# Two kinds of expert weight blocks taken by turns, with other PSUM homes, in a two-block transformer kernel

## Chip, core and metric

One core of a Trainium2 chip runs the whole program. The metric is device time in microseconds (us), the median of three timed runs. Beside it stands one profiled execution, from which every row below is taken.

## What is computed

Two small transformer blocks, 256 tokens of width 1024, one after the other, all in float32. The part that matters is the mixture of experts at the end of the first block:

```python
def moe_swiglu(h, router_w, w1, w3, w2):          # cut: the sorting of tokens
    top_val, top_idx = lax.top_k(h @ router_w, 2)  # 2 of 8 experts for each token
    gates = softmax(top_val)
    # for every expert e, over the tokens that chose it (xb):
    y = (silu(xb @ w1[e]) * (xb @ w3[e])) @ w2[e]  # 1024 -> 2816 -> 1024
    # each token adds its two y, weighted by its gates
```

Each expert has three matrices of 1024 x 2816 (or its transpose), 34.6 MB in float32, and all eight are read from HBM: 276.8 MB of the kernel's 505 MB.

## The kernel before

**The experts' stage.** Experts are ordered by how many tokens chose them. The first three (`NL = 3`) have slots for 128 tokens and are computed with three products: every weight chunk is split into a rounded part `hi` (ScalarE, L325) and the rest `lo` (VectorE, L326), and TensorE multiplies hi by hi, hi by lo and lo by hi. The other five have slots for 64 tokens and are plain: TensorE reads the float32 chunk as it landed (`raw`), with 64 columns, two tiles of the array at a time.

**Chunks and places.** Weights arrive in chunks of 1 MiB, two DMAs of 512 KB each; an expert is 33 chunks (11 each of w1, w3, w2). A *place* `(e, f)` is one block of columns of one expert. A three-product expert has six places: five of 6 chunks (4 for w1 and w3, 2 for w2), and one of 3. A plain expert has three: two of 12 chunks (8 and 4), and one of 9. `moe_steps()` lists the places in order. For each, `up` multiplies by w1 and w3 (tiles `H`, L1417 or plain L1434), ScalarE and VectorE form the gated product `mg` (L1443, L1444), `gtrans` transposes it on TensorE (`gTp`, L1455 or L1464) and `down` multiplies by w2 into `Y` (L1483) or `Ys` (L1497). The `down` of a place comes after the `up` of the next place, and its `gtrans` between w1 and w3 of the next place.

**Buffers and queues.** `stream()` fixes the order of the chunks; SyncE (SP) issues all their DMAs in that order, each into the next free home. There are 7 homes of one chunk for raw chunks in this stage (3 from the start, 2 + 2 from `more_raw`). A home of a three-product chunk is free when its split is done, that of a plain chunk when TensorE has read it. `hi` and `lo` hold three chunks, and two are split ahead of use (`look = 2`). Once the last three-product chunk (`i_three`) is done with, the `hi` and `lo` buffers too are homes for plain chunks, 6 more. Two further chunks go to tiles that are still unused at the stage's start.

**Background work.** `gather` selects an expert's tokens (tiles `xgp`, `STp`, `gsp`), `gather_plain` those of the five plain experts at once, `combine` and `combine_plain` add an expert's result to the residual `hT` (tile `sc`). They are generators: one step of each active one runs at a `tick`, one tick a chunk or so.

**The turn.** Between the three-product and the plain part stands `moe_rest`, a branch for experts with more tokens than slots, which is not taken here; all engines read a count and pass it.

**PSUM** has 8 banks of 128 x 512 float32: tags `mm` 3, `st` 1, `Y` 2, `ac` 2. A tag without banks of its own (`gT`) falls to `ac`. The instruction order on each engine is that of a scheduler inside the framework, which may place an instruction later than the code has it.

Of the kernel before, what the change touches and what calls it, by code (L numbers as in the profile page):

```python
# [8 lines left out]
F32R = mybir.dt.float32r  # L9
# [8 lines left out]
T = 256  # L18
# [3 lines left out]
NE = 8  # L22

NL = 3
RMS_EPS = 1e-6
LN_EPS = 1e-5
BIG = 1e30
# [29 lines left out]

def moe_steps():

    return [(e, f) for e in range(NL) for f in range(6)] + [(e, f) for e in range(NL, NE) for f in range(3)]  # L60


def up_keys(nm, e, f):
# [13 lines left out]
def stream():  # L77

    ch = []

    def pack(key, nm, i, parts):
        ch.append((key, [128, KD, sum(n for _, n in parts)], [(nm, i, 0, D, c, n) for c, n in parts]))

    def cols(key, nm, i, c0, n=256):
        pack(key, nm, i, [(c0, n)])

    def rows(key, nm, i, r0, n=256):
        ch.append((key, [128, n // 128, D], [(nm, i, r0, n, 0, D)]))  # L90

    for i in range(6):
        cols(("ain", i), "a_w_in", (0,), 256 * i)
    for i in (8, 10, 9, 11, 6, 7):
        cols(("ain", i), "a_w_in", (0,), 256 * i)
    for i in range(4):
        cols(("aout", i), "a_w_out", (0,), 256 * i)
    for f in range(12):
        if f < 11:
            cols(("f1", f), "ffn_w1", (0,), 256 * f)  # L100
            cols(("f3", f), "ffn_w3", (0,), 256 * f)
        if f > 0:
            rows(("f2", f - 1), "ffn_w2", (0,), 256 * (f - 1))
    rows(("pple", 0), "ple_proj", (0,), 0)
    for i in range(4):
        cols(("gple", 0, i), "ple_gate", (0,), 256 * i)
    for i in (4, 5, 6, 7, 0, 1, 2, 3):
        cols(("cin", i), "c_w_in", (0,), 256 * i)
    for i in range(4):
        cols(("cout", i), "c_w_out", (0,), 256 * i)  # L110
    shapes = {c[0]: c[1] for c in experts()}
    prev = None
    for e, f in moe_steps():
        down = down_keys(*prev) if prev else []
        up = up_keys("m1", e, f) + up_keys("m3", e, f)
        ch += [(k, shapes[k[0], k[2], k[3]], None) for k in (down + up if (e, f) == (NL, 0) else up + down)]
        prev = e, f
    ch += [(k, shapes[k[0], k[2], k[3]], None) for k in down_keys(*prev)]
    rows(("pple", 1), "ple_proj", (1,), 0)
    for i in range(4):  # L120
        cols(("gple", 1, i), "ple_gate", (1,), 256 * i)
    for l in range(2):
        for n, parts in enumerate((
                [(512, 128), (704, 128)], [(640, 64), (832, 32), (1504, 12), (384, 128)], [(0, 256)],
                [(256, 128), (1120, 128)], [(864, 256)], [(1248, 64), (1376, 64), (1312, 64), (1440, 64)],
                [(1516, 256)], [(1772, 256)], [(2028, 256)])):
            pack((f"c{n}", l), "w_in_2", (l,), parts)
        for i in range(4):
            cols(("wout", l, i), "w_out_2", (l,), 256 * i)
        for f in range(17):  # L130
            if f < 16:
                cols(("up", l, f), "w_up_2", (l,), 256 * f)
            if f > 0:
                rows(("dn", l, f - 1), "w_down_2", (l,), 256 * (f - 1))
    return ch
# [45 lines left out]
class Prog:  # L181
# [986 lines left out]
    def moe(self, nxt):  # L1168
        nc, a = self.nc, self.a
# [17 lines left out]
        x = self.nx[0:2]  # L1187
# [1 line left out]
        xtk = [self.xt(f"xtk{q}").rearrange("p (s b k) t -> p s b (k t)", s=2, b=2) for q in range(2)]  # L1189

        def rows(s, b, q, f):
            ps = self.ac("xtp", (128, 512), F32R)
            for j in range(4):
                nc.tensor.transpose(ps[:, 128 * j:128 * j + 128], x[s][:, 4 * q + j, 128 * b:128 * b + 128],
                                    self.identr)
            return f(xtk[q][:, s, b], ps.bitcast(F32))
# [152 lines left out]
        def gather(e):  # L1349
            S = slots((e,)) if e else first  # L1350
            last = [None, None]
            g = self.p_x.tile([128, 2, KD, 128], F32R, tag="X", name="xg")
            for i in range(2):
                for s in range(2):
                    ps = self.psum("ac" if s or e else "mm", "xgp", (128, 4, 128))
                    for j in range(4):
                        for b in range(2):
                            nc.tensor.matmul(ps[:, j], xtk[i][:, s, b, 128 * j:128 * j + 128], S[:, b, 0],
                                             start=b == 0, stop=b == 1)
                    o = g[:, s, 4 * i:4 * i + 4]  # L1360
                    if s:
                        last[0] = nc.scalar.activation(o, ps, AF.Copy)
                    else:
                        last[1] = nc.vector.tensor_copy(o, ps)
                    yield
            if not e:
                with self.after(*last):
                    ghl.append(gates())
            ST, gs = slotsT(S, (e,), ghl[0])
            xg[e] = g[:, 0], g[:, 1]  # L1370
            sg[e] = ST[:, 0], gs[:, 0]

        def gather_plain():

            g = self.big("xs", [128, KD, NE - NL, 64])
            for e0 in range(NL, NE, 3):
                es = range(e0, min(e0 + 3, NE))
                n = len(es)
                S = slots(es, plain=True)
                yield  # L1380
                for k in range(KD):
                    ps = self.ac("xgp", (128, n, 64))
                    for s in range(2):
                        for b in range(2):
                            nc.tensor.matmul(ps, xtk[k // 4][:, s, b, 128 * (k % 4):128 * (k % 4) + 128],
                                             S[:, b, :, 0:64], start=s == 0 and b == 0, stop=s == 1 and b == 1)
                    o = g[:, k, e0 - NL:e0 - NL + n]
                    if k % 2:
                        nc.scalar.activation(o, ps, AF.Copy)
                        yield  # L1390
                    else:
                        nc.vector.tensor_copy(o, ps)
                q = slotsT(S, es, ghl[0], f"s{e0}")
                for m, e in enumerate(es):
                    xg[e] = g[:, :, e - NL]
                    sg[e] = q[0][:, m], q[1][:, m]
# [4 lines left out]
        G, Y = {}, {}  # L1401
# [46 lines left out]

        def gtrans(e, f):
            t = G.pop((e, f))  # L1450
            ps = self.psum("gT", "gTp", (128, 4, 128))
            if e < NL:
                nf = 4 if f < 5 else 2
                for j in range(nf):
                    nc.tensor.transpose(ps[:, j], t[:, 128 * j:128 * j + 128], self.ident)  # L1455
                hi = p.tile([128, 4, 128], F32R, tag="gth", name="gth", bufs=2)
                lo = p.tile([128, 4, 128], F32R, tag="gtl", name="gtl", bufs=2)
                self.hilo(hi[:, :nf], lo[:, :nf], ps[:, :nf])
                GT[e, f] = hi, lo
                return  # L1460
            gt = p.tile([128, 4, 128], F32, tag="gth", name="gts", bufs=2)
            for j in range(4):
                c = 128 if f < 2 or j < 2 else 64
                nc.tensor.transpose(ps[:, j, :c], t[:c, 128 * j:128 * j + 128], self.ident[:c, :c])  # L1464
            if f < 2:
                nc.vector.tensor_copy(gt, ps)
            else:
                nc.vector.tensor_copy(gt[:, 0:2], ps[:, 0:2])
                nc.vector.tensor_copy(gt[:, 2:4, 0:64], ps[:, 2:4, 0:64])
            GT[e, f] = gt  # L1470
# [53 lines left out]
        def combine_plain(e):  # L1524
# [4 lines left out]
            nc.scalar.activation(t, Y.pop(e), AF.Identity, scale=gs[:, 0:1])  # L1529
            yield  # L1530
            for i in range(2):
                P = [self.ac("sc", (128, 2, T)) for _ in range(2)]
                for j in range(2):
                    c = 256 * i + 128 * j
                    for q in range(2):
# [11 lines left out]

        prev = None
        for e, f in steps:
            if (e, f) == (NL, 0):  # L1550
                gtrans(*prev)
                down(*prev)
                self.drain()
# [2 lines left out]
                self.moe_rest(xtk, cni, slots, slotsT, ghl[0])  # L1556
                prev = None
            up(e, f, prev)
            if e < NL and f == 1:
                self.add(gather(e + 1) if e < NL - 1 else gather_plain())  # L1560
            if prev:
                down(*prev)
                if f == 0:
                    self.add((combine if e <= NL else combine_plain)(e - 1))
            prev = e, f
        gtrans(*prev)
        down(*prev)
# [4 lines left out]
    def moe_rest(self, xtk, cni, slots, slotsT, ghl):  # L1572
# [4 lines left out]
        with tc.If(n > 128):  # L1577
# [20 lines left out]
            for e, off in [(e, 128) for e in range(NL)] + [(e, o) for e in range(NL, NE) for o in (64, 192)]:  # L1598
                S = slots((e,), off)
                ST, gs = slotsT(S, (e,), ghl)  # L1600
                P = [self.ac("P20"), self.ac("P21")]
                for i in range(2):
                    for j in range(4):
                        for s, ps in enumerate(P):
# [509 lines left out]
    def build(self):  # L2114
# [24 lines left out]
                self.rows = True  # L2139
                self.mods(32)  # L2140
        self.dump("h4", self.hT)
        with self.more_raw("raw3", "left", 2), self.phase("moe", 1, Y=2, ac=2):
            self.moe((self.col("ln_ple", 1),))
        raw2.__exit__(None, None, None)
        self.dump("h5", self.hT)
# [77 lines left out]
```

## Time and profile before

| | |
|---|---|
| median of three runs | 1873.13 us (1872.68 to 1876.75) |
| the profiled execution's own time | 1875.38 us |
| its span, first to last instruction | 1873.6 us |
| experts' stage, first `H` to the last `Ys` matmul | 442.9 to 1162.5 us |
| three-product part of it | 442.9 to 756 us |
| plain part | 762.6 to 1162.5 us |

How to read it: the span is what rows of the trace add up to, the run's own time is 1.8 us more, and the three timed runs lie around it. A matmul's end is modelled, so its busy time overlaps with the next one's; the step from start to start is what one costs.

### The profile page before, as it was taken

What the parts mean: (1) busy time and instruction counts of PE and PEld (TensorE: products, weight loads), DVE (VectorE), ACT (ScalarE), POOL (GpSimd) and SP (SyncE); (2) the same over time, 40 slices, a digit from 0 to 9 for tenths busy, and PEclk for the clock granted to TensorE, in tenths of its full rate; (3) what the DMA queues carried; (4) which work ended last, traced back from release to release, by engine and by line L of the source; (5) the groups of instructions that cost most, each with busy time, mean ns of one, the idle gap of its engine ahead of it and who ended that gap; (6) DMA issues with size and microseconds to landing.
All of it is one profiled execution on the core that took longest, in us unless ns stands there. A gap on an engine that the chain in (4) does not pass through costs nothing.

```text
span 1873.6 us, 31611 instructions
## 1 busy us (share of the span) xinstructions
PE 1768.3 (94%) x11889; PEld 1428.9 (76%) x11889; DVE 1176.8 (63%) x2150; ACT 909.2 (49%) x1428; POOL 53.0 (3%) x93
## 2 busy tenths in 40 slices
PE   7999999999999999899898888999999999999998
PEld 7989999997888888333232223887899998889997
DVE  7888888687899988101000011886888877666554
ACT  6754435666787866000000002666555456666553
POOL 1000000000000000000000000200000000000000
PEclk9999999998999999999999999999999999999999
DMA  8479886575899989999999999443588864326651
GB/s 308 144 261 315 309 308 218 185 246 210 297 361 330 368 299 326 376 413 412 413 412 413 412 413 383 163 155 106 209 307 303 314 215 138 113 69 204 190 185 53
DMA packets 138544, 508.55 MB, mean 271 GB/s; under 512 B 18192, under 2 KB 18832, under 8 KB 137872
## 3 DMA queue, kind: packets, MB, share of 16 engines
q1 hardware_dynamic: 132480, 496.92, 73.0%
q10 hardware_dynamic: 5904, 9.53, 1.6%
q8 instruction: 96, 1.57, 0.3%
q14 instruction: 64, 0.52, 0.1%
HBM read 505.34 MB, written 1.05 MB: 270 GB/s over the span
## 4 chain that ended last, share of the span: by engine, by line
PE 31%; DMA 22%; DVE 4%; ACT 2%; issue 1%; SPq 0%; DVEq 0%; ACTq 0%
DMA raw<-in_moe_dram 19%; PE y L632 8%; PE up L406 7%; PE zp L406 5%; DMA adaw<-in_ada_dram 2%; PE H L1434 2%; PE S L1839 2%; DVE lo L326 1%; PE op L406 1%; PE pTp L1045 1%; PE cmh L1946 1%; PE oT L1873 1%; ACT hi L325 1%; DVE adacc L865 1%; PE op L431 1%
## 5 line engine op out<-in xcount | busy, mean ns | idle before, releaser
L326 DVE TENSOR_TENSOR lo<-raw,hi 128x1024 fp32r<-128x1024 f32 x516 | 621.8, 1223 | 131.5 <-ACT hi L325 130.0
L325 ACT ACTIVATE hi<-raw 128x1024 fp32r<-128x1024 f32 x516 | 530.9, 1054 | 185.6 <-PE H L1417 38.2
L1434 PE MATMUL H<-raw,xs 128*64 128x512 f32 (+1 forms) x960 | 229.7, 567 | 39.3 <-DMA raw<-in_moe_dram 32.7
L1434 PEld LDWEIGHTS H<-raw,xs 128*64 128x64 f32 x960 | 75.1, 137 | 182.7 <-issue 97.8
L1444 DVE SCALAR_TENSOR_TENSOR mg<-H,gs,mg 128x512 f32<-128x512 f32 (+3 forms) x38 | 26.3, 692 | 290.1 <-PE H L1434 198.7
L632 PE MATMUL y<-ghi,hi 128*128 128x256 f32 x688 | 193.6, 283 | 3.9 <-ACT ghi L377 3.7
L632 PE MATMUL y<-ghi,lo 128*128 128x256 f32 x688 | 194.0, 282 | 2.0 <-DVE lo L326 2.0
L632 PE MATMUL y<-glo,hi 128*128 128x256 f32 x688 | 194.0, 282 | 1.9 <-DVE glo L378 1.9
L1417 PE MATMUL H<-hi,xg 128*128 128x512 f32 (+1 forms) x576 | 178.1, 382 | 0.0
L1443 ACT ACTIVATE mg<-H,gs 128x512 f32<-128x512 f32 (+3 forms) x38 | 24.2, 636 | 307.0 <-PE H L1434 306.9
L865 DVE SCALAR_TENSOR_TENSOR adacc<-adaw,cact,adacc 128x768 f32<-128x768 f32 x126 | 130.9, 1039 | 47.7 <-DMA adaw<-in_ada_dram 46.0
L406 PE MATMUL up<-xhi,hi 128*128 128x258 f32 x480 | 136.3, 284 | 0.2 <-ACT hi L325 0.2
L406 PE MATMUL up<-xhi,lo 128*128 128x258 f32 x480 | 135.6, 283 | 0.0
L406 PE MATMUL up<-xlo,hi 128*128 128x258 f32 x480 | 135.4, 282 | 0.0
L632 PEld LDWEIGHTS y<-ghi,hi 128*128 128x128 f32 x688 | 129.9, 189 | 5.0 <-ACT ghi L377 4.9
L632 PEld LDWEIGHTS y<-glo,hi 128*128 128x128 f32 x688 | 130.3, 189 | 2.9 <-DVE glo L378 2.9
L632 PEld LDWEIGHTS y<-ghi,lo 128*128 128x128 f32 x688 | 130.2, 189 | 2.6 <-DVE lo L326 2.6
L1497 PE MATMUL Ys<-raw,gts 128*64 128x512 f32 x440 | 119.4, 606 | 8.6 <-DMA raw<-in_moe_dram 7.1
L1417 PEld LDWEIGHTS H<-hi,xg 128*128 128x128 f32 x576 | 105.9, 189 | 20.7
L1417 PE MATMUL H<-lo,xg 128*128 128x512 f32 (+1 forms) x288 | 108.9, 378 | 0.0
L406 PE MATMUL H<-xhi,lo 128*128 128x256 f32 x336 | 94.7, 282 | 0.0
L406 PE MATMUL H<-xhi,hi 128*128 128x256 f32 x336 | 94.3, 281 | 0.0
(604 smaller groups left out, 3820.2 us busy)
## 6 DMA issues: line engine op xcount, KB each, us to landing
raw<-in_moe_dram SPq DMA_DIRECT2D x524, 512.0 KB, 10.0
raw<-in_stream_dram SPq DMA_DIRECT2D x316, 512.0 KB, 4.5
adaw<-in_ada_dram SPq DMA_DIRECT2D x64, 768.0 KB, 6.4
cw1k<-in_cw1k_dram ACTq DMA_DIRECT2D x2, 1024.0 KB, 6.4
cw1v<-in_cw1v_dram ACTq DMA_DIRECT2D x2, 1024.0 KB, 5.5
raw<-in_stream_dram SPq DMA_DIRECT2D x4, 472.0 KB, 4.5
hT<-in_xT_dram SPq DMA_DIRECT2D x4, 256.0 KB, 7.2
raw<-in_stream_dram ACTq DMA_DIRECT2D x2, 512.0 KB, 7.6
```

What stands on the lines that cost most here:

```text
L325: self.halved = (nc.scalar.activation(hi, raw, AF.Copy), nc.vector.tensor_sub(lo, raw, hi.bitcast(F32)))
L326: nc.vector.tensor_sub(lo, raw, hi.bitcast(F32)))
L406: nc.tensor.matmul(ps, p[:, k, j:j + m], q[:, k, :], start=start and n == 0, stop=n == 3 * nk - 1, skip_group_check=True)
L431: nc.tensor.matmul(ps, p[:, k, c:c + m[n]], q[:, k, :], start=k == i == 0 and not (n and shared), stop=k == KD - 1 and i == 2, skip_group_ ...
L632: self.nc.tensor.matmul(ps, p[:, k, 128 * dt:128 * dt + 128], q[:, k, :], start=f == 0 and n == 0 and dt % 2 == 0, stop=last and n == 5, s ...
L865: nc.vector.scalar_tensor_tensor(acc, w[:, j], self.cact[:, k:k + 1], acc, op0=OP.mult, op1=OP.add)
L1417: nc.tensor.matmul(ps[:, :n], g[s][:, m // 3], w[:, k], start=m == 0, stop=m == 23, skip_group_check=True)
L1434: nc.tensor.matmul(ps[64 * q:64 * q + 64, :c], g[:, k], x[:, kk], start=k == 0, stop=k == KD - 1, skip_group_check=True)
L1443: nc.scalar.activation(t[z, :c], H[0][z, :c], AF.Silu, scale=gs[z, 1:2])
L1444: nc.vector.scalar_tensor_tensor(t[z, :c], H[1][z, :c], gs[z, 1:2], t[z, :c], op0=OP.mult, op1=OP.mult)
L1497: nc.tensor.matmul(Y[e][64 * q:64 * q + 64], gt[:, kk, 64 * n:64 * n + 64], w[:, k, 512 * q:512 * q + 512], start=key[2] == 0 and kk == 0, ...
L1839: nc.tensor.matmul(S[n][:, c:c + b], q[n][:, a:a + 128], k[n][:, 0:b], start=True, stop=True)
```

## The change

The order of places is new. Expert 0 stands alone, six places. Then come twelve pairs: a plain place of experts 3 to 6, and a three-product place of experts 1 and 2. Expert 7 (plain) is last, and the turn (`MOE_REST`) stands before it. The plain gather therefore comes during expert 0. In PSUM `Y` has 3 banks and `ac` 1; `gTp` moves from `ac` to `mm`, one of the two `sc` tiles of `combine_plain` to `mm`, and other tiles between `Y`, `ac` and `mm`. `gather_plain` yields after every block and not after every second. Amounts of data, of products and of splits are the same.

```diff
+MOE_REST = (NE - 1, 0)
 def moe_steps():
-    return [(e, f) for e in range(NL) for f in range(6)] + [(e, f) for e in range(NL, NE) for f in range(3)]
+    a = [(e, f) for e in range(1, NL) for f in range(6)]
+    b = [(e, f) for e in range(NL, NE) for f in range(3)]
+    r = [(0, f) for f in range(6)]
+
+    for x, y in zip(b, a):
+        r += [x, y]
+    assert b[len(a)] == MOE_REST
+    return r + b[len(a):]
...
-            ps = self.ac("xtp", (128, 512), F32R)
+            ps = self.psum("Y", "xtp", (128, 512), F32R)
...
-                    ps = self.psum("ac" if s or e else "mm", "xgp", (128, 4, 128))
+                    ps = self.psum("ac" if e else "Y", "xgp", (128, 4, 128))
...
                         nc.scalar.activation(o, ps, AF.Copy)
-                        yield
                     else:
                         nc.vector.tensor_copy(o, ps)
+                    yield
...
-            ps = self.psum("gT", "gTp", (128, 4, 128))
+            ps = self.mm("gTp", (128, 4, 128))
...
-                P = [self.ac("sc", (128, 2, T)) for _ in range(2)]
+                P = [self.psum(t, "sc", (128, 2, T)) for t in ("ac", "mm")]
...
-            if (e, f) == (NL, 0):
+            if (e, f) == MOE_REST:
...
             up(e, f, prev)
-            if e < NL and f == 1:
-                self.add(gather(e + 1) if e < NL - 1 else gather_plain())
+            if (e, f) == (0, 1):
+                self.add(gather_plain())
+            if (e, f) in [(0, 4)] + [(n, 1) for n in range(1, NL - 1)]:
+                self.add(gather(e + 1))
             if prev:
                 down(*prev)
-                if f == 0:
-                    self.add((combine if e <= NL else combine_plain)(e - 1))
+                if prev[1] == (5 if prev[0] < NL else 2):
+                    self.add((combine if prev[0] < NL else combine_plain)(prev[0]))
...
-        with self.more_raw("raw3", "left", 2), self.phase("moe", 1, Y=2, ac=2):
+        with self.more_raw("raw3", "left", 2), self.phase("moe", 1, Y=3, ac=1):
```

What this makes of the instruction order is seen best where a plain place gives way to a three-product place. Before, in the middle of expert 2, VectorE's queue holds the splits (`lo`, line L326, two rows a chunk) in an even row, with the gated product `mg` (L1444) between the halves of one chunk:

```order
L326 TENSOR_TENSOR lo<-raw_6967,hi 128x1024
L1444 SCALAR_TENSOR_TENSOR mg<-H,gs,mg 128x512
L326 TENSOR_TENSOR lo<-raw_6968,hi 128x1024
L326 TENSOR_TENSOR lo<-raw_6994,hi 128x1024
L326 TENSOR_TENSOR lo<-raw_6995,hi 128x1024
L326 TENSOR_TENSOR lo<-raw_7018,hi 128x1024
```

After the change, VectorE's queue in a pair (the lines are numbered 9 higher: L335 is the split, L1453 `mg`, L387 and L1475 the copies of `gTp`; the first `mg` is that of the plain place):

```order
L387 TENSOR_TENSOR gtl<-gTp,gth 128x512
L1453 SCALAR_TENSOR_TENSOR mg<-H,gs,mg 128x512
L335 TENSOR_TENSOR lo<-raw_7751,hi 128x1024
L335 TENSOR_TENSOR lo<-raw_7752,hi 128x1024
L335 TENSOR_TENSOR lo<-raw_7763,hi 128x1024
L335 TENSOR_TENSOR lo<-raw_7764,hi 128x1024
L335 TENSOR_TENSOR lo<-raw_7775,hi 128x1024
L1475 COPY gts<-gTp 128x512
L335 TENSOR_TENSOR lo<-raw_7776,hi 128x1024
L335 TENSOR_TENSOR lo<-raw_7787,hi 128x1024
```

All splits of the run of three-product chunks now stand behind the plain place's `mg`, none ahead of it. TensorE's queue at the same place, where the last plain `H` matmuls (on chunks 7735 and 7748) meet the first of the three-product `down` (`Y`, L1492):

```order
L1443 MATMUL H<-raw_7735,xs 64x512
L1443 MATMUL H<-raw_7748,xs 64x512
L1443 MATMUL H<-raw_7735,xs 64x512
L1443 MATMUL H<-raw_7748,xs 64x512
L1492 MATMUL Y_6980<-hi,gth 128x512
L1492 MATMUL Y_6981<-hi,gth 128x512
L1492 MATMUL Y_6980<-lo,gth 128x512
L1492 MATMUL Y_6980<-hi,gtl 128x512
```

So the plain `H` must be complete, `mg` formed and the first chunk split before more than two of the `Y` matmuls can run.

## Rows read from the trace of the kernel before

**Rows 1.** The page, part 2: GB/s moved in 40 equal slices of 46.8 us.

```profile
GB/s 308 144 261 315 309 308 218 185 246 210 297 361 330 368 299 326 376 413 412 413 412 413 412 413 383 163 155 106 209 307 303 314 215 138 113 69 204 190 185 53
```

**Rows 2.** Busy time by stretch: us, busy us (instructions) by engine, granted clock, DMA share, GB/s.

```profile
540.00:640.00 100.00, 100.00 (x495) 83.48 (x494) 90.46 (x89) 76.93 (x85) 0.00 (x0) 1.00 0.95 346
...
742.00:763.00 21.00, 13.01 (x62) 9.83 (x62) 7.51 (x11) 4.33 (x7) 0.23 (x2) 0.91 0.84 311
...
929.00:1014.00 85.00, 73.00 (x309) 23.41 (x308) 7.31 (x12) 3.21 (x5) 0.00 (x0) 1.00 1.03 413
```

**Rows 3.** Waits of SP's queue, 443 to 742 us: total us, times, longest.

```profile
SPq L310 <- DVE lo L326: 167.5, 165, 6.5
```

**Rows 4.** The same for 780 to 1160 us.

```profile
SPq L310 <- DMA raw<-in_moe_dram: 220.7, 294, 2.1
```

**Rows 5.** Timeline of TensorE, plain experts: start us, us, instruction, count.

```profile
929.24 0.49 PE L1537 MATMUL sc<-ST,ys 64*128 64x256 f32 x2
...
1014.22 0.49 PE L1537 MATMUL sc<-ST,ys 64*128 64x256 f32 x2
...
1163.35 0.49 PE L1537 MATMUL sc<-ST,ys 64*128 64x256 f32 x2 [0.85 <-ACT ys L1529]
```

**Rows 6.** Timeline of TensorE: first matmul of experts 0, 1 and 2.

```profile
442.90 0.76 PE L1417 MATMUL H<-hi,xg 128*128 128x512 f32 x1
...
539.91 0.39 PE L1417 MATMUL H<-hi,xg 128*128 128x512 f32 x1
...
640.20 0.39 PE L1417 MATMUL H<-hi,xg 128*128 128x512 f32 x1
```

**Rows 7.** Timeline of TensorE just behind the turn, chunks landed ahead.

```profile
785.60 7.09 PE L1434 MATMUL H<-raw,xs 128*64 128x512 f32 x32
...
800.28 0.59 PE L1434 MATMUL H<-raw,xs 128*64 128x512 f32 x2
```

**Rows 8.** Groups on TensorE, 640 to 742 us, with the plain gather: busy us, mean ns, idle.

```profile
L1385 PE MATMUL xgp<-S,xtk 128*128 128x192 f32 (+1 forms) x64 | 8.2, 270 | 0.0
L1455 PE MATMUL gTp<-ident,mg 128*128 128x128 f32 x22 | 3.5, 278 | 1.9 <-DVE xs L1392 1.9
L1340 PE MATMUL STp<-identr,S 128*128 128x128 f32 x10 | 1.2, 256 | 0.0
```

**Rows 9.** Groups on TensorE, 763 to 1160 us: four plain combines.

```profile
L1537 PE MATMUL sc<-ST,ys 64*128 64x256 f32 x64 | 11.8, 408 | 0.0
L1464 PE MATMUL gTp<-ident,mg 128*128 128x128 f32 (+1 forms) x60 | 10.9, 286 | 3.4 <-DVE hT L1540 3.1
```

**Rows 10.** The page, part 5: the split and the gated product, mean ns second.

```profile
L326 DVE TENSOR_TENSOR lo<-raw,hi 128x1024 fp32r<-128x1024 f32 x516 | 621.8, 1223 | 131.5 <-ACT hi L325 130.0
L325 ACT ACTIVATE hi<-raw 128x1024 fp32r<-128x1024 f32 x516 | 530.9, 1054 | 185.6 <-PE H L1417 38.2
...
L1443 ACT ACTIVATE mg<-H,gs 128x512 f32<-128x512 f32 (+3 forms) x38 | 24.2, 636 | 307.0 <-PE H L1434 306.9
```

**Rows 11.** Timeline of TensorE at the turn.

```profile
748.00 0.38 PE L1455 MATMUL gTp<-ident,mg 128*128 128x128 f32 x2
...
762.57 1.12 PE L1434 MATMUL H<-raw,xs 128*64 128x512 f32 x2 [6.32 <-PEq L1577]
```

**Rows 12.** Busy time by stretch, columns as in Rows 2.

```profile
762.00:766.00 4.00, 3.43 (x8) 1.14 (x10) 0.00 (x0) 0.00 (x0) 0.23 (x2) 0.50 1.05 418
...
780.00:1160.00 380.00, 335.82 (x1446) 109.67 (x1444) 33.23 (x55) 14.68 (x23) 0.00 (x0) 1.00 1.03 412
```

**Rows 13.** Waits of the weight loads for chunks, 763 to 1160 us: total us, times, longest.

```profile
PEld H L1434 <- DMA raw<-in_moe_dram: 75.5, 74, 3.1
```

**Rows 14.** DMA queue 1 and issues, 500 to 540 us: packets, MB, share; KB, us to landing.

```profile
q1 hardware_dynamic: 4076, 14.83, 100.2%
...
raw<-in_moe_dram SPq DMA_DIRECT2D x27, 512.0 KB, 5.4
```

**Rows 15.** Issues, 800 to 840 us.

```profile
raw<-in_moe_dram SPq DMA_DIRECT2D x32, 512.0 KB, 10.0
```

More of the change, by code (lines that the diff above doesn't have):

```diff
@@ L115, in stream @@
         up = up_keys("m1", e, f) + up_keys("m3", e, f)
-        ch += [(k, shapes[k[0], k[2], k[3]], None) for k in (down + up if (e, f) == (NL, 0) else up + down)]
+        ch += [(k, shapes[k[0], k[2], k[3]], None) for k in (down + up if (e, f) == MOE_REST else up + down)]
         prev = e, f
@@ L1600, in moe_rest @@
                 ST, gs = slotsT(S, (e,), ghl)
-                P = [self.ac("P20"), self.ac("P21")]
+                P = [self.ac("P20"), self.psum("Y", "P21")]
                 for i in range(2):
```

## Prediction

> **What bounds the kernel now.** I read the 40 slices first [rows 1]: between slices 10 and 24 the core moves 297 to 376 GB/s, then holds 412 without a break. These are the two parts of the experts' stage. By stretches [rows 2], the three-product part has TensorE busy for all of its 100 us at 346 GB/s; the plain part has DMA at 413 GB/s and TensorE busy 73 of 85 us. The waits of SP's queue confirm it: in the first part it waits for `lo`, that is for a home to be emptied by a split (167.5 us) [rows 3], in the second for earlier DMAs to land (220.7 us) [rows 4]. So one part wastes bandwidth and the other wastes TensorE.
>
> Prices. A plain expert takes 1014.22 - 929.24 = 85.0 us for 33 chunks [rows 5]: 2.576 us a chunk, the pace of DMA. A three-product expert takes 640.20 - 539.91 = 100.3 us [rows 6], 3.04 us a chunk, TensorE's pace, with one gather and one combine in it. What TensorE alone needs for a plain expert is seen behind the turn, where chunks lie ready [rows 7]: 7.09 us for one matrix of a place, and 800.28 - 785.60 = 14.7 us for that, a transposition and the `down`. A place of 12 chunks is then 7.1 + 14.7 = 21.8 us, one of 9 about 20.2 (its `down` has 3 chunks for 4), an expert 64 us.
>
> **The change, part by part.** Data, products and splits stay. What moves is which limit meets which.
>
> *Expert 0 alone.* It took 539.91 - 442.90 = 97.0 us [rows 6]. The plain gather comes into it: 8.2 us of `xgp`, 1.2 of `STp`, about as much for the small matmuls beside them (my estimate), and 1.9 us of idle [rows 8], 12.5 in all. Pairs begin at 442.9 + 109.5 = 552.4 us. With one `ac` bank each `xgp` waits for the copy of the one before; a chunk's matmuls lie between, so I cost that at nothing beyond the 1.9. Without that cover it would be at most one split, 1.22 us [rows 10], for 16 blocks: 20 us.
>
> *Twelve pairs, TensorE's account.* Expert 1 as before: 100.3. Expert 2 without a gather (32 matmuls, half of the `xgp` above, and its small ones, 4.6 together): 95.7. Four plain experts: 256. Three of their combines: (11.8 + 3.4) / 4 = 3.8 each [rows 9], 11. New is the point where a plain place gives way to a three-product place. The queues printed above have every split behind the plain place's `mg`, so TensorE waits for one `mg` on ScalarE, one `hi` and one `lo`: 0.64 + 1.05 + 1.22 = 2.9 us [rows 10], less two matmuls that need no `lo`: 2.4 us, twelve times, 29. Below that is 0, if TensorE waits for data there anyway; above it the whole first chunk, 4.2 us. I take 2.4, since the rows of both queues say so. Sum 492 us. `lo` takes 2.45 us a chunk against TensorE's 3.04, so later splits keep ahead.
>
> *The same, DMA's account.* 198 chunks x 2.576 = 510 us, less the 7 chunks in homes when the pairs begin, 18: 492 us. The accounts are equal by chance. Where two limits alternate each loses something: a three-product place with the wait lasts about 17.4 + 2.4 = 20 us, in which DMA could bring 7.7 chunks for 6 used up; with all homes full, as in the first pairs, that surplus is lost, 4 us each time. I add 10 us (0 to 25): 502, to 1054.8 us.
>
> *The turn.* From the last transposition at 748.00 to 762.57 it took 14.6 us [rows 11]. One plain combine joins, 3.8: 18.4, to 1073.2 us. DMA lost (412 - 311) / 412 x 21 = 5 us there [rows 2].
>
> *Expert 7.* TensorE needs 64 us and the clock stood at half, 1.2 GHz, for 4 us behind the turn [rows 12], which costs 2: 1139 us. By DMA: 39 chunks had landed at 552.4, the other 225 need 579.6, the turn 5, the last chunk 1.8: also 1139. Both accounts have slack of their own to lose, so I add 4: 1143 us. Before, the last `Ys` ended at 1162.5 (1163.35 less the 0.85 of waiting) [rows 5]. What follows is unchanged. **Gain 19.5 us**: the profiled execution goes from 1875.4 to 1855.9. That one stands 2.3 above the median of the runs, so the median goes to 1853.6.
>
> **A rule against it.** The sum needs 412 GB/s while ScalarE and VectorE split, which the three-product part never showed. It held 370 at best (14.83 MB in 40 us, 500 to 540), with the queue's packets covering 100.2% of the 16 engines' time [rows 14], which reads like a full DMA. But a DMA landed 5.4 us after its issue there and 10.0 in the plain part [rows 15]: half as many were under way. I take the queue as often empty there, and 412 as open to the pairs. The Trainium skill, "DMA: Bandwidth & Descriptors", section "Where 436 GB/s comes from", says that HBM binds loads to SBUF at about 358 GB/s a core. This trace does not agree: 412 GB/s over 380 us [rows 12]. By the rule the six experts of the pairs would need 207.6 MB / 358 = 580 us instead of 510, and the kernel would be some 50 us slower than before; by the row the sum stands.
>
> **Rivals.**
> 1. *DMA is full at 370 GB/s beside the splits.* For it: the 100.2%. Against it: the landing times, and TensorE busy all the time in that stretch. The pairs then take 510 x 412 / 370 - 20 = 548 us, 46 more: 1900 us, slower. It decides at 20 us more than my 502, a pace of 2.74 us a chunk or 383 GB/s. The page's rule above would act in this way.
> 2. *Each pair waits more than I count*: one `ac` bank, `sc` in `mm` where `H` lives, copies behind splits in VectorE's queue. For it: the gather already idled TensorE 1.9 us with two banks [rows 8]. Against it: in plain places VectorE has almost nothing to do (7.3 of 85 us) [rows 2]. At 1 us a pair the gain is 8 (1866); at 1.6 it is gone.
> 3. *The clock falls at the new waits.* TensorE idled 6.32 us at the turn and ran at 1.2 GHz for 4 us afterwards [rows 11, 12], 2 us of work lost. Twelve times that is 24 us: 1878, slower; it decides at 1.6 us a wait. Against it: the plain part is full of waits, up to 3.1 us [rows 13], and the clock was 1.00 from 780 to 1160 [rows 12]. The Trainium skill, "TensorE: Matmul & The Clock Gate", section "Why this matters for your kernels", warns that idle gaps between bursts let the clock drop; this trace agrees at the turn and shows none in the plain part.
> 4. *All fits*: no loss where the limits meet, and SP passes the turn early, as before. 39 chunks landed at 552.4 and 225 to come give 1132, the last one's work 1134: gain 29, 1844.
> 5. *Nothing comes of it*: if 7 homes are too few for 12 plain chunks in a row (before, 13 were open to them), DMA runs in bursts as in the first part. Against it: a DMA lands 10.0 us after its issue, 4 chunks, and TensorE holds 2. At the first part's 346 GB/s the six experts take 207.6 MB / 346 - 20 = 580 us, 78 more than my 502: 1932. A quarter of it gives no change.
>
> **How the numbers follow.** My forecast (1841 to 1863) has 0.58, rival 2 with a smaller gain 0.14 and overshot 0.03, rival 1 0.08, rival 3 0.04, rival 4 beyond 1841 0.05, and no change, by rivals 2 or 5, 0.05; the remaining 0.03 is rival 5's slower form. A measurement of this kernel tells about 0.2%, 3.7 us, from no change. Faster: 0.58 + 0.14 + 0.05 = 0.77. Same 0.05. Slower 0.18. The predicted time is the forecast's, 1853.6. The range goes from 1839, a little under rival 4's 1844, to 1877, over which the slower forms of rivals 1, 3 and 5 lie: it leaves out about 0.2. The forecast's own range is 1841 to 1863.
>
> **What would show it.** Right: 400 GB/s or more in the middle of the pairs; twelve waits of 2 to 3 us on the first `Y` matmul of three-product places; pairs of 42 to 47 us; the last `Ys` at about 1143; pairs from about 552; SP waiting for landings there and no longer for `lo`; a clock of 1.00 but for the turn. Wrong: 370 GB/s with landings at 10 us (rival 1), `xgp`, `sc` or `gTp` with several us of idle before them (2), clock rows at 0.5 in the pairs (3), or SP waiting for `H` and `Ys` reads with few DMAs under way (5).

## The result

The kernel got slower. The time after the change is 1885.6 us (median, 1885.05 to 1892.62) beside 1872.9 for the kernel before in the same runs: a ratio of 1.0079, 95% interval 1.0054 to 1.0105, some 13 to 15 us more. The prediction was 1853.6, range 1839 to 1877, with a chance of 0.18 for slower.

The profiled execution after has a span of 1883.3 us. First the page, part 2, GB/s in 40 slices of 47.1 us, which answers to [rows 1]:

```profile
GB/s 308 141 255 298 314 317 223 191 250 199 287 264 366 349 375 376 413 383 373 381 378 415 414 353 413 205 140 132 166 307 313 306 244 143 111 69 202 185 188 54
```

The pairs fill slices 13 to 23 of the 40: 349 to 383 GB/s in eight of them, 413 to 415 in three. The 412 without a break that the plain part had is gone. By stretches, with the columns of [rows 2]:

```profile
560.00:600.00 40.00, 40.00 (x192) 22.49 (x190) 18.30 (x22) 13.16 (x16) 0.00 (x0) 1.00 1.03 413
600.00:640.00 40.00, 36.05 (x148) 19.54 (x146) 17.56 (x17) 13.96 (x15) 0.00 (x0) 1.00 0.74 280
640.00:680.00 40.00, 36.75 (x163) 20.00 (x159) 16.80 (x17) 14.93 (x16) 0.00 (x0) 1.00 0.93 368
960.00:1000.00 40.00, 37.67 (x154) 19.61 (x152) 17.82 (x17) 13.88 (x14) 0.00 (x0) 1.00 0.94 371
1000.00:1040.00 40.00, 33.59 (x141) 16.16 (x138) 13.48 (x13) 12.22 (x13) 0.00 (x0) 0.96 1.03 414
```

In the three rows between the first and the last TensorE is busy 36 to 38 of 40 us and DMA moves 280 to 371 GB/s: neither limit is reached. The places in time come from TensorE's timeline (as in [rows 5, 6, 11]): the first plain `H`, where the pairs begin; the last three-product transposition, where they end; expert 7's first `H`; its last `Ys`.

```profile
551.74 1.51 PE L1443 MATMUL H<-raw,xs 128*64 128x512 f32 x6
...
1085.80 0.44 PE L1464 MATMUL gTp<-ident,mg 128*128 128x128 f32 x2
...
1107.37 1.12 PE L1443 MATMUL H<-raw,xs 128*64 128x512 f32 x2 [3.04 <-PEq L1588]
...
1173.86 1.08 PE L1506 MATMUL Ys<-raw,gts 128*64 128x512 f32 x4 [0.20 <-DMA raw<-in_moe_dram]
```

| step | forecast | measured |
|---|---|---|
| pairs begin | 552.4 | 551.7 |
| pairs last | 502 | 534.1 |
| the turn lasts | 18.4 | 21.6 |
| expert 7 lasts | 66 and 4 | 67.6 |
| last `Ys` ends | 1143 | 1174.9 |

Before, the last `Ys` ended at 1162.5. One step is off by much: the pairs, by 32 us. The waits of SP's queue in them, 552 to 1089 us (total us, times, longest):

```profile
SPq L319 <- DMA raw<-in_moe_dram: 192.9, 247, 5.8
SPq L319 <- PE H L1443: 61.7, 31, 10.1
SPq L319 <- DVE lo L335: 54.2, 32, 8.2
SPq L319 <- PE Ys L1506: 16.1, 29, 1.8
```

Beside landings SP waits 54 us for splits and 78 us for plain chunks to be read; in the plain part before, landings were what counted [rows 4]. What happens is seen at one place where a plain run gives way to a three-product run, 660 us. TensorE's timeline, then VectorE's:

```profile
657.59 2.42 PE L1443 MATMUL H<-raw,xs 128*64 128x256 f32 x9
660.00 0.73 PE L1492 MATMUL Y<-hi,gth 128*128 128x512 f32 x2
662.07 0.51 PE L1492 MATMUL Y<-lo,gth 128*128 128x512 f32 x1 [1.33 <-DVE lo L335]
```

```profile
660.14 0.74 DVE L1453 SCALAR_TENSOR_TENSOR mg<-H,gs,mg 64x512 f32<-64x512 f32 x1 [13.32 <-PE H L1443]
660.81 1.21 DVE L335 TENSOR_TENSOR lo<-raw,hi 128x1024 fp32r<-128x1024 f32 x1
662.05 0.49 DVE L1453 SCALAR_TENSOR_TENSOR mg<-H,gs,mg 64x256 f32<-64x256 f32 x1
662.57 3.50 DVE L335 TENSOR_TENSOR lo<-raw,hi 128x1024 fp32r<-128x1024 f32 x3
```

TensorE has two matmuls to do and waits for `lo`: 2.07 us from the first `Y` to the first that needs `lo`, where two matmuls take 0.46 (1.6 lost, eleven such waits in the pairs). That is the wait that was priced at 2.4. (The place is one of nine chunks, where `mg` has two parts, and the first `lo` stands between them.) The other side is SP's, 650 to 663 us:

```profile
SPq L319 <- DMA raw<-in_moe_dram: 7.9, 4, 5.8
SPq L319 <- DVE lo L335: 3.1, 1, 3.1
```

For 9 us on end SP issues nothing: first 5.8 us for a landing, then 3.1 for a `lo`. The landing that ends the first wait, at 658.8 us, is that of a load issued at 648.8. So SP waits to load into the home of a chunk that is itself still on its way and has then to be split. DMA's rate from 560 to 1040 us, in 40 slices of 12 us, shows the same at turn after turn:

```profile
GB/s 410 417 412 302 118 374 417 415 268 404 415 412 264 411 415 416 409 415 414 412 416 414 408 290 408 415 393 286 418 412 315 382 414 414 300 386 416 414 414 413
```

### The profile page after: what moved, and what is told of

Read it like the earlier page. It is cut to its first block, busy times and chain, and to the rows that moved or that the text cites. A ratio compares the mean times of both kernels' runs of the same rounds, so it can differ in the third digit from the quotient of the medians.

```text
span 1883.3 us, 31543 instructions
## 1 busy us (share of the span) xinstructions
PE 1784.8 (95%) x11889; PEld 1430.7 (76%) x11889; DVE 1178.1 (63%) x2150; ACT 911.2 (48%) x1428; POOL 52.7 (3%) x93
## 5 line engine op out<-in xcount | busy, mean ns | idle before, releaser
L335 DVE TENSOR_TENSOR lo<-raw,hi 128x1024 fp32r<-128x1024 f32 x516 | 621.9, 1226 | 150.3 <-ACT hi L334 148.3
L1443 PE MATMUL H<-raw,xs 128*64 128x512 f32 (+1 forms) x960 | 230.1, 569 | 15.8 <-DMA raw<-in_moe_dram 12.7
L1453 DVE SCALAR_TENSOR_TENSOR mg<-H,gs,mg 128x512 f32<-128x512 f32 (+3 forms) x38 | 26.4, 694 | 196.9 <-PE H L1443 160.6
L1426 PE MATMUL H<-lo,xg 128*128 128x512 f32 (+1 forms) x288 | 114.0, 396 | 7.6 <-DVE lo L335 7.5
L1506 PE MATMUL Ys<-raw,gts 128*64 128x512 f32 x440 | 111.8, 599 | 1.5 <-DMA raw<-in_moe_dram 1.3
```

Source lines behind the costliest of these rows:

```text
L335: nc.vector.tensor_sub(lo, raw, hi.bitcast(F32)))
L1426: nc.tensor.matmul(ps[:, :n], g[s][:, m // 3], w[:, k], start=m == 0, stop=m == 23, skip_group_check=True)
L1443: nc.tensor.matmul(ps[64 * q:64 * q + 64, :c], g[:, k], x[:, kk], start=k == 0, stop=k == KD - 1, skip_group_check=True)
L1453: nc.vector.scalar_tensor_tensor(t[z, :c], H[1][z, :c], gs[z, 1:2], t[z, :c], op0=OP.mult, op1=OP.mult)
L1506: nc.tensor.matmul(Y[e][64 * q:64 * q + 64], gt[:, kk, 64 * n:64 * n + 64], w[:, k, 512 * q:512 * q + 512], start=key[2] == 0 and kk == 0, ...
```

## The experiments

The theories. **A** (homes): at the turns SP can't issue because homes are not free, DMA stands, and plain runs starve later. **B**: TensorE's own waits at the turns, and single PSUM banks, bound the pairs. **C**: the new PSUM homes cost the time. Times are ratios to the kernel before, run beside each. Two kernels with equal pairs differed by 8 us in the median (see the promises below), so besides the ratio I read two stretches of each profile: the pairs as above, and the stage, from expert 0's first `H` to the end of the last `Ys`.

| run | median us | ratio, interval | pairs | stage |
|---|---|---|---|---|
| before | 1873.1 | | | 719.6 |
| after | 1885.6 | 1.0079, 1.0054 to 1.0105 | 534.1 | 731.9 |
| psum_only | 1869.9 | 1.0008, 0.9996 to 1.0020 | | 720.8 |
| before_h6 | 1873.6 | 1.0041, 1.0026 to 1.0056 | | 724.4 |
| h6 | 1887.9 | 1.0121, 1.0104 to 1.0139 | 535.5 | 736.7 |
| split_first | 1870.6 | 1.0009, 0.9995 to 1.0023 | 515.7 | 716.7 |
| home_order | 1862.1 | 0.9957, 0.9938 to 0.9977 | 510.3 | 708.2 |
| promise1 | 1853.9 | 0.9929, 0.9904 to 0.9954 | 511.7 | 709.2 |
| both | 1852.5 | 0.9910, 0.9895 to 0.9925 | 497.5 | 700.9 |
| both_promise1 | 1853.7 | 0.9917, 0.9901 to 0.9934 | 501.7 | 702.7 |
| both_h6 | 1855.3 | 0.9938, 0.9918 to 0.9959 | 506.3 | 706.4 |
| straight | 1848.0 | 0.9883, 0.9859 to 0.9906 | 496.4 | 701.1 |
| fine | 1890.7 | 1.0113, 1.0097 to 1.0130 | 530.8 | 735.4 |
| fine_home | 1888.3 | 1.0109, 1.0093 to 1.0126 | 525.2 | 735.6 |

**The PSUM edits alone** (psum_only): the kernel before, with these and the other PSUM edits of the diff, but its own order of places.

```diff
-            ps = self.psum("gT", "gTp", (128, 4, 128))
+            ps = self.mm("gTp", (128, 4, 128))
-                P = [self.ac("sc", (128, 2, T)) for _ in range(2)]
+                P = [self.psum(t, "sc", (128, 2, T)) for t in ("ac", "mm")]
-        with self.more_raw("raw3", "left", 2), self.phase("moe", 1, Y=2, ac=2):
+        with self.more_raw("raw3", "left", 2), self.phase("moe", 1, Y=3, ac=1):
```

> The old order of places with all of the change's PSUM edits (Y 3 banks, ac 1, gTp in mm, sc in ac and mm, xtp, xgp and P21 in their new homes, the plain gather yielding after every block). Theories A and B: within 5 us of the kernel before, 1870 to 1878 us. Theory C (the PSUM homes by themselves cost the time): 1883 us or more.

No change: 1.0008. Theory C falls. The three-product part and a plain expert run as in [rows 2]:

```profile
540.00:640.00 100.00, 99.69 (x491) 82.88 (x491) 89.96 (x88) 76.92 (x84) 0.00 (x0) 1.00 0.96 345
929.00:1014.00 85.00, 73.98 (x310) 23.68 (x308) 7.31 (x12) 3.21 (x5) 0.00 (x0) 1.00 1.03 413
```

**A home less** (h6, and before_h6 as its control, with the same 2 made 1).

```diff
-        with self.more_raw("raw3", "left", 2), self.phase("moe", 1, Y=3, ac=1):
+        with self.more_raw("raw3", "left", 1), self.phase("moe", 1, Y=3, ac=1):
```

> The kernel after with 6 homes for raw chunks in place of 7. Theory A (homes): DMA halts one chunk earlier at each of the twelve turns, 12 x 2.58 = 31 us if nothing of it is made up; 1900 to 1920 us. Theory B (TensorE's waits) and theory C (PSUM homes): the waits named there do not hang on the number of homes; within 6 us of 1885.

> The kernel before with 6 homes in place of 7, the control for the run above. Theory A: the three-product part is bound by TensorE (3.04 us a chunk against DMA's 2.58), and the plain part has 12 homes: 1873 to 1880 us. If the time rises by 20 us or more here too, a home less is costly whatever the order, and the run above says nothing on the pairs.

A home less costs 0.42% after (1.0121 against 1.0079) and 0.41% before, 8 us each. The expected 15 us or more did not come, and the pairs hardly moved (535.5). About half of what is lost lies behind them: expert 7 lasts 71.7 us for 67.6. So theory A in this form, too few homes, falls: in the kernel after it isn't their number.

**mg behind the splits** (split_first): the plain place's `mg` waits in the queues of ScalarE and VectorE for the first two chunks' splits.

```diff
+            ahead = [i for i in self.parts if not self.plain(i)]
+            with self.after(*(self.halved if e >= NL and ahead else ())):
...
                     nc.scalar.activation(t[z, :c], H[0][z, :c], AF.Silu, scale=gs[z, 1:2])
```

> The kernel after, with the plain place's gated product mg held behind the splits of the next two three-product chunks. Theory A (homes: the late splits keep all 7 homes full at the turn from a plain to a three-product place, DMA stands still there and the plain places starve later): two homes come free during the plain place, the 22.5 us in which DMA stands still in the pairs mostly go, pairs end about 25 to 33 us sooner, time 1850 to 1862 us, DMA 400 GB/s or more in all of the pairs' 40 us windows. Theory B (TensorE's own waits at the turns, 12 times 2.1 us, and the single PSUM banks bound the pairs): at most those 25 us, with DMA's pace still in bursts and SP waiting as long for homes as before. Theory C (the new PSUM homes cost the time): no change, 1885 us.

1870.6: 13 us won, half of what A expected, and SP still waits (50.0 us for `H`, longest 10.1; 34.0 for `lo`, longest 4.5). That is what B expected: at most 25 us, with DMA still in bursts. From 560 to 1040 us TensorE's waits on the first `Y` fell from 13.5 to 3.0 us, those for chunks only from 12.7 to 11.2. DMA still dips, in the slices as above:

```profile
GB/s 403 416 413 325 205 411 415 412 307 417 414 393 327 416 414 414 411 416 413 414 413 416 413 414 414 415 299 416 415 345 365 416 414 346 405 417 414 414 413 413
```

The code then gave a sharper theory. `pump` writes the splits of up to two chunks ahead of use (`look = 2`), and a split that is only *written* into the program already gives its chunk's home to the next load (`leave`, called in `_split`). At a turn two such splits are written while the last two plain chunks still hold their homes. So the next two loads go into the homes of chunks that have not landed, and stand in SP's queue ahead of loads that could go where the plain chunks were. I call that a home promised (theory A2; A1 is the short supply whatever the order).

**The order of homes** (home_order: after with this edit alone; both: with mg behind the splits too).

```diff
     def may_split(self):
         if self.i_split not in self.raws or self.plain(self.i_split):
             return self.i_split in self.raws
+        if self.got or any(self.plain(i) for i in self.parts):
+            return False
```

> The kernel after; only the order in which homes are given out differs: while a plain chunk still occupies a home, no three-product chunk's home is promised to a later load, so that the loads at the turn take the homes of the last plain chunks first. The order on ScalarE, VectorE and TensorE stays, with mg ahead of the splits. Theory A2 (the load that stands first in SP's queue at the turn waits for a split that ends last, while homes of plain chunks are free): SP's longest waits at the turns (6 to 9 us) shrink by about 4 us each, DMA loses some 20 us less in the pairs, 1868 to 1876 us; TensorE's 2.1 us at the turns stay. Theory A1 (7 homes are too few, whichever comes first): 1883 to 1888 us. Theory B (TensorE's own waits): 1885 us.

> The run before this one together with mg held behind the first two chunks' splits. Theory A2: the gains add up, 1852 to 1862 us, with the dips in DMA's rate at the turns gone. Theory A1: 1868 to 1873, what holding mg back gave by itself (1870.6). Theory B: the same as A1.

The order of homes alone takes the kernel from 1.0079 to 0.9957, 1.2% or 23 us, some 6 us below the 1868 to 1876 that A2 expected. VectorE's and ScalarE's instructions in the stage stand in the same order in both traces, `mg` first at the turns; TensorE's waits there are unchanged, while its waits for chunks are gone. Waits of TensorE in home_order, 560 to 1040 us:

```profile
PE Y L1494 <- DVE lo L335: 13.9, 10, 1.4
PE H L1428 <- DVE lo L335: 3.7, 8, 0.5
PE sc L1548 <- ACT ys L1540: 2.3, 3, 0.8
```

The kernel after has in the same stretch, on top:

```profile
PE H L1443 <- DMA raw<-in_moe_dram: 12.7, 12, 2.9
```

SP's waits in home_order, 552 to 1063 us, and DMA's rate in the slices as above:

```profile
SPq L319 <- DMA raw<-in_moe_dram: 96.8, 145, 1.9
SPq L319 <- PE H L1445: 89.9, 71, 10.1
SPq L319 <- DVE lo L335: 57.0, 76, 2.8
SPq L319 <- PE Ys L1508: 52.5, 73, 3.4
```

```profile
GB/s 405 415 413 415 393 367 328 415 412 410 329 374 418 398 384 413 414 416 412 418 411 410 398 413 383 418 414 413 416 414 413 402 345 416 414 356 418 414 411 419
```

The longest wait for a landing falls from 5.8 to 1.9 us, that for a `lo` from 8.2 to 2.8. The 10.1 us for `H` stay, and in all SP waits little less (296 us for 325), but in shorter pieces, and no slice of DMA's falls below 328 GB/s. With both edits the time is 1852.5, ratio 0.991, within the 1852 to 1862 expected by A2. The pairs fall by 23.8 us through the order of homes and by 12.8 more through mg: A2 has the larger part of the loss, and B, TensorE's own waits (which the forecast counted), the smaller. The run both, in stretches, and DMA's rate in the slices as above:

```profile
640.00:720.00 80.00, 78.53 (x337) 41.99 (x335) 36.05 (x37) 29.01 (x31) 0.00 (x0) 1.00 1.02 411
720.00:800.00 80.00, 79.07 (x378) 41.87 (x376) 30.94 (x33) 25.59 (x29) 0.00 (x0) 1.00 1.03 414
800.00:880.00 80.00, 76.02 (x326) 39.82 (x324) 35.72 (x37) 27.52 (x31) 0.00 (x0) 1.00 1.03 415
880.00:960.00 80.00, 77.99 (x342) 42.03 (x339) 35.12 (x37) 29.36 (x32) 0.00 (x0) 1.00 1.03 415
960.00:1040.00 80.00, 75.67 (x343) 39.52 (x344) 29.81 (x31) 24.27 (x27) 0.00 (x0) 1.00 1.03 416
```

```profile
GB/s 416 414 414 415 396 407 335 415 415 413 389 414 412 417 414 411 418 412 418 413 414 417 413 414 416 415 414 415 416 412 416 415 416 415 415 417 416 414 418 415
```

One slice, 335, is left below 340 where eight stood below 320. At a turn of this kernel, 651 us, SP waits for plain `H` reads, six short waits of at most 1.2 us (640 to 655 us), and VectorE has split two chunks before `mg`. SP's waits, then VectorE's timeline:

```profile
SPq L319 <- PE H L1445: 7.0, 6, 1.2
```

```profile
645.41 3.72 DVE L335 TENSOR_TENSOR lo<-raw,hi 128x1024 fp32r<-128x1024 f32 x3 [5.63 <-ACT hi L334]
649.94 1.23 DVE L335 TENSOR_TENSOR lo<-raw,hi 128x1024 fp32r<-128x1024 f32 x1 [0.81 <-ACT hi L334]
651.59 1.27 DVE L1457 SCALAR_TENSOR_TENSOR mg<-H,gs,mg 64x512 f32<-64x512 f32 x2 [0.43 <-PE H L1445]
```

**One promise in place of two** (promise1: after with this; both_promise1: split_first with this).

```diff
-        return len([i for i in self.parts if not self.plain(i)]) < self.look and \
+        held = self.got or any(self.plain(i) for i in self.parts)
+        return len([i for i in self.parts if not self.plain(i)]) < (1 if held else self.look) and \
```

> The kernel after, where, while a plain chunk occupies a home, the home of one three-product chunk (in place of two, or of none as in the run on the order of homes) is promised to a later load. If the first promise blocks SP's queue for all loads behind it (head of the line), nearly the whole loss stays: 1878 to 1886 us. If each promised home costs by itself, half of the 23 us is won: 1872 to 1875. If TensorE's turns were the loss: 1885.

> Held-back mg as in the first run, and the home of one three-product chunk (two there, none in the best version) promised to a later load while a plain chunk occupies a home. With TensorE's waits at the turns the promise of one cost nothing, but there TensorE had no wait for chunks left, so that a loss of DMA's could hide. The pairs' stage, first plain H to last Y, was 524.6 us with two promised and 506.4 with none. If one promise blocks the loads behind it as two do: 518 to 525 us, time 1864 to 1871. If the loss is in the second promise, since with one the next loads go into the last plain chunks' homes: 505 to 511 us, time 1851 to 1857.

The idea that the first promise blocks everything behind it fell, and so did the half of 23 us for each: with one promise the pairs last 511.7 us, as with none (510.3), and the time is 1853.9, below every range expected. With TensorE's waits taken away too it is 501.7 against 497.5 with none and 515.7 with two. So with `mg` held back one promise costs some 4 us, the second 14 more, by one profile of each. (To the last `Y`, the measure of the expectation, both_promise1 took 510.5.) The two medians, 1853.9 and 1862.1 with equal pairs, come from outside: in the profiles 4.4 us lie ahead of expert 0 and 8.9 behind the last `Ys`.

**A home less in the best version** (both_h6: both, with the line of h6).

> The best version so far (order of homes, and mg behind the splits; 1852.5) with 6 homes for 7. A home less cost 8 us in both earlier pairs of runs. If, with the homes given out in the right order, 7 are about enough, as theory A2 has it: 1855 to 1863 us, still faster than the kernel before. If homes are short whatever their order (A1): 1870 or more.

0.9938: 5 us lost, still faster than before; the pairs take 506.3 us for 497.5. With the homes given out in this order, 6 are nearly enough.

**Finer turns** (fine, fine_home): runs of 4 plain and 2 three-product chunks. `up` makes one matrix now, and `gated` forms `mg`, held back as in split_first; `pl` is a pair's plain and three-product place, `todo` the two places before. `stream()` follows the same order, `gTp` lies in `ac`, and a few other tiles have other homes or numbers of buffers. The core of the edit:

```diff
-            up(e, f, prev)
+            for nm in ("m1", "m3"):
+                for x in pl:
+                    if todo and (nm, x) != ("m1", pl[0]):
+                        gtrans(*todo.pop(0))
+                    H[nm, x] = up(nm, *x, tag="st" if len(pl) == 2 and (nm, x) == ("m3", pl[1]) else "mm")
+                    if nm == "m3":
+                        gated(*x, (H["m1", x], H["m3", x]))
```

Both of these runs leave out the combine of expert 6 at the turn, so their times are some 4 us too short.

> The same pairs in finer turns: w1 of the plain place, w1 of the three-product place, w3 of the one, w3 of the other, then both downs; runs of 4 plain and 2 three-product chunks by turns in place of 12 and 6. mg is off TensorE's path (its transposition comes in the next pair), and is held behind the splits. If what a long run lacks or has over in chunks is the loss (theory A1): 400 GB/s or more throughout, pairs of 500 to 508 us in place of 538, 1848 to 1858 us. If the promise of homes to loads is it (A2): three times as many turns with the same wait for a split, no better than 1870. If TensorE's waits at the turns were all (B): 1860.

> The finer turns with the order of homes of the first run of this group. Theory A2: 1848 to 1858 us and clearly below the finer turns alone. Theory A1: within 3 us of the finer turns alone.

1.0113 and 1.0109: no faster than the kernel after. A1's 400 GB/s did not come, but here TensorE is the limit, so the runs say little of A1; A2's 1848 to 1858 for fine_home missed. In fine TensorE is busy 76 of 80 us, and yet does fewer matmuls (297 recorded from 800 to 880 us, 326 in both), with DMA at 374 GB/s:

```profile
800.00:880.00 80.00, 76.07 (x297) 37.07 (x294) 32.17 (x36) 27.26 (x32) 0.00 (x0) 0.98 0.95 374
```

**A clean change between the kinds** (straight: both, and `Ys` held until the last three-product `H`).

```diff
+                        with self.after(self.last):
                             nc.tensor.matmul(Y[e][64 * q:64 * q + 64], gt[:, kk, 64 * n:64 * n + 64],
```

> The best version so far, and the first plain Ys matmuls of a place held until the last three-product H matmul: in 8 of the 12 turns two Ys matmuls stand between the last six H matmuls, and in the trace the two then take 1.00 us in place of 0.44, with some 0.1 us more behind them. Theory S (each change between the two kinds of matmul costs TensorE about a third of a microsecond, which is what made the finer turns slow): TensorE wins 8 x 0.6 = 5 us; as DMA runs at 415 GB/s there already, 0 to 5 us of it show: 1847 to 1853 us, and the change from H to Ys takes about 0.33 us once. Without theory S: the same time, and the same 1.00 us for the first two Ys matmuls.

The change from `H` to `Ys` in both, then in straight:

```profile
668.02 1.07 PE L1510 MATMUL Ys<-raw,gts 128*64 128x512 f32 x2
669.03 0.50 PE L1428 MATMUL H<-lo,xg 128*128 128x512 f32 x1
...
670.06 0.40 PE L1428 MATMUL H<-hi,xg 128*128 128x512 f32 x1
```

```profile
672.85 0.40 PE L1428 MATMUL H<-hi,xg 128*128 128x512 f32 x1
673.18 0.65 PE L1511 MATMUL Ys<-raw,gts 128*64 128x512 f32 x2
```

In both, two `Ys` stand between the last `H` matmuls, and it takes 1.01 us from the first of them to the next `H`, where two of a row take 0.44. In straight the change is one step of 0.33 us, where a step in a row of `H` is 0.23. So the 1.01 us is gone, as S has it, but a clean change costs 0.1 us and not a third. In time S is not told apart: 0.9883 and 0.9910 with overlapping intervals, pairs 496.4 and 497.5, stages 701.1 and 700.9. Straight is the lowest of all and beats both kernels, by 1.2% and 1.9%. Fine has two more changes there and back in each pair. In its trace 24 `H` and 32 plain matmuls with a pair of plain ones between the `H` take 14.0 us (685.95 to 699.95), at the steps of a row 12.6; 1.4 us, 24 times, would be about the 33 by which its pairs are longer than those of both. This is an estimate from one stretch, and no run tested it: why the finer turns lose stays open.

## Why the prediction was wrong

Point by point, by its own steps.

- *Expert 0 alone*: right, 551.7 for 552.4. The plain gather fitted in.
- *Twelve pairs, TensorE's account*, 492 us: too small. Home_order shows it alone, since TensorE waits for no chunk there: 510.3, 18 more. The wait at the turn itself was right in place, and 1.6 us each where I took 2.4, 9 less in all; so the work was some 27 us too small. Part of it is the gather of expert 2: the plain run that holds it lasted 32.2 us there, from its first `Ys` to the next `Y`, the like one without it 23.2, so 9 us where I took 4.6. The three plain runs with a combine lasted 27.8 us each, of which five `H` take 1.2; by my prices 24.0, so 8 us in all. Part are the changes between kinds, by an estimate up to 1 us a pair, which I left out. The rest I have not broken down.
- *Where two limits alternate*, "I add 10 us (0 to 25): 502": **this is the step that failed.** The pairs took 534.1. Of the 32 us too many, 24 vanish with the order of homes alone, and the remaining 8 are the 18 above less the 10 added. I had the surplus lost with "all homes full", and treated the 7 homes as alike. In the program they are not: a load takes a home by name, SP issues in order, and at each turn two loads were bound to chunks that had yet to land and be split. The text said that every split stands behind `mg`, but asked only what TensorE loses by it, not which load waits for the home. With that put right and `mg` moved, the pairs take 497.5 us and the kernel 1852.5, beside 502 and 1853.6 forecast. That nearness is in part luck: the 502 holds 29 us of waits at the turns, of which both has 2.2, in place of the work that I had too small; and expert 7 lasts 74.7 us there, not 70. (The sum's 1054.8 should be 1054.4; it changes nothing.)
- *The turn*: 21.6 for 18.4. `combine` now has one bank, and its matmuls wait for the addition of the block before; psum_only, with the old order, shows it too, 17.2 us for 14.6. TensorE's timeline after:

```profile
1099.52 0.38 PE L1528 MATMUL sc<-ST,yh 128*128 128x256 f32 x1 [0.78 <-DVE hT L1530]
...
1101.13 0.55 PE L1528 MATMUL sc<-ST,yh 128*128 128x256 f32 x1 [0.87 <-DVE hT L1530]
```

- *Expert 7*: 67.6, within the 66 and 4.
- Rival 1, DMA full at 370 GB/s beside the splits: wrong. The run both holds 411 to 416 GB/s for 400 us with splits running. The Trainium skill, "DMA: Bandwidth & Descriptors", section "Where 436 GB/s comes from", binds loads at about 358 GB/s a core; these traces do not agree, in the pairs as little as in [rows 12].
- Rival 2: `sc` waits 3.1 us in all pairs; not it. Rival 3: in the pairs of the kernel after the clock fell once, to half (1.2 GHz), at the end of a wait of 2.94 us for a chunk, at 1011.4 us; 32 plain matmuls then took 8.68 us for 7.09 [rows 7]. At 1.6 us in all it isn't the cause. Rival 4, no loss where the limits meet: wrong, by the 534.1.
- Rival 5 named the sign that came, SP waiting for `H` reads with DMA in bursts, but put it down to 7 homes being too few. In both_h6, with the homes in order, even 6 cost only 9 us of pairs.

## What to carry to other kernels

When two kinds of work alternate on one in-order load queue, ask of each buffer which earlier use it is bound to, and when that use ends; a count of free buffers says nothing of a load that stands first in the queue and is bound to the wrong one. Freeing a buffer in the program when its consumer is written, and not when it is likely to run, was harmless in the steady three-product part before, where TensorE was busy all the time [rows 2], and costly where the kind changes. Price what an interleaving adds at its seams (the wait, the load behind it, the change of kind), times the number of seams, before its averages.

## What the runs showed of the hardware

DMA's rate takes some time to come back after such a halt. At the turn at 660 us, in slices of 2 us from 640 us on, the rate falls to 84 GB/s and passes 400 again only in the fifth slice behind that (the kernel after):

```profile
GB/s 416 418 414 412 412 414 424 414 404 340 84 147 268 367 340 410 408 420 422 422 424 401 420 418 412 416 401 418 414 422 397 422 422 315 20 270 268 287 383 414
```

Part of this is SP's doing: its first load goes out at 662.0 us and lands 3.2 us later, the second goes out at 663.8, after one more wait for a `lo`, and the next ones 0.5 us and more apart. How much is DMA's own, no run tells.

And a pair of plain matmuls between three-product ones costs more than its own time: 1.01 us for 0.44. In a row they start two at a time (in straight the first two 0.01 us apart at 673.18), while the pair that stands alone in both starts 0.48 us apart (668.02 and 668.50). Why it does so is not shown.
